# Down-projection of a streaming-encoder block: a ring of three weight chunks, one place for block sums, a fixed chunk order, and an end by products

## The chip, the cores and the metric

One core of a Trainium2 chip runs the whole kernel. The metric is device time in microseconds of one launch. The engines are TensorE (PE, with its weight loads PEld), VectorE (DVE), ScalarE (ACT), GpSimd (POOL) and SyncE (SP), which here only issues DMAs.

## What is computed

A block of a hybrid encoder on x of 512 frames by 1024: two attention branches, mixed into x, then a gated unit (ConvGLU) with its own residual. The change is in the last matrix product, `@ w_down`, of 2816 rows:

```python
def conv_glu(x, w_up, conv_w, conv_b, w_down):
    hid = x @ w_up
    ...
    gate, up = hid[..., :D_FF], hid[..., D_FF:]
    return (jax.nn.silu(gate) * up) @ w_down
...
x = x + conv_glu(rms_norm(x, norm2_g[l]), w_ffn_up[l], ...)
```

## The kernel before

Every product is done in float32 by three matmuls: each operand is split into a high part (a cast to a narrower type, by ScalarE: `hi`, tiles `whi`) and a residual (VectorE: `lo`, tiles `wlo`), and TensorE adds high x high, high x low and low x high. In `down_body` these are lines 855, 856 and 857.

The down-projection is done by Strassen's method in Winograd's form: 7 products in place of 8 block products. It has two sweeps, one for each half of 512 output columns, and in each sweep 11 chunks (`dn{s}_{i}`; sweep s, chunk i), one for each pair of 128-row blocks of `w_down`. The activation side (`pairs[i]`, tiles `a`) was made in the stage before. A chunk of weights has four raw blocks of 256 columns (128x1024, 512 KB), and three more blocks that are sums of them (`down_sums`, lines 111 to 113, VectorE). Three products take a raw block (1, 3 and 2), four take a sum (5, 7, 6 and 4). A chunk is 7 products x 2 row tiles x 3 = 42 matmuls, and each product adds up over the 11 chunks in a PSUM bank of its own; there are 8 banks.

How a chunk is prepared (`split_gen`): while TensorE works on chunk i, ScalarE casts chunk i+1 in two pieces (line 131: 768 columns of raw blocks, then 1024 with the sums), VectorE makes the two residuals (line 133), and SyncE then loads chunk i+2 (line 100). Raw tiles, `whi` and `wlo` have two buffers each. So a cast of chunk i+1 waits until TensorE has left chunk i-1, and a load waits until the residuals of two chunks before are done. A raw tile is 2048 wide: the left half holds the weights, the right half the chunk's own block sums.

At the end of a sweep (`fin`, `sweep`) the seven products are combined with x2, the block's input to this stage, which lies in DRAM (`x2d`). SyncE loads x2's columns for a sweep with chunk 6 of that sweep into one tile `xo` (line 870), VectorE adds the products to it as they end (line 884), in the order 1, 6, 5, 7, 2, 4, 3, and SyncE stores it (lines 878 and 915). Both sweeps use the same tile, so the loads of the second wait for the stores of the first.

A scheduler sets the order on each engine from the program's order and its own estimate of times; `behind(a, b)` forces a after b on one engine without a wait.

## Time and profile before

| | us |
|---|---|
| runs (3) | 748.29, 748.57, 749.75; median 748.57 |
| profiled execution | 750.49 |
| its span, first to last instruction | 747.8 |
| granted TensorE clock, mean | 0.996 |
| first matmul of the down-projection to its last (starts) | 626.3 to 740.5 |

The profile's columns are the engines' busy times. A row of the timeline has the start, the duration, engine, line, operation, tiles and shapes; in brackets stands the engine's idle time before it and what ended that. A row with x2 is two instructions with the sum of their time from the first's start to the last's end. The chain of waits leads back from the last instruction to what released each step.

### The profile page before, as it was taken

The page shows a single profiled execution, that of the slowest core. Times are in us where ns is not written, and L with a number is a line of the kernel's source. Part 1 is how long each engine was busy: PE and PEld are TensorE (multiplying, and loading weights), DVE is VectorE, ACT ScalarE, POOL GpSimd, SP SyncE. Part 2 cuts the span into 40 slices and gives each one's busy share as a digit, 9 for nine tenths or more (in the row PEclk, how much of TensorE's full clock was granted, in tenths as well). Part 3 has the DMA queues.
Part 4 walks back from the last instruction along what each step waited for, and adds up shares of the span by engine and source line. Part 5 has one row for each costly group of instructions (what it writes and reads, how often), then busy time and mean ns, then how long its engine had stood idle before and what let it go on. Part 6 is the DMA issues. An engine that isn't in the chain of part 4 may idle for free.

```text
span 747.8 us, 10959 instructions
## 1 busy us (share of the span) xinstructions
PE 733.1 (98%) x4301; PEld 645.1 (86%) x4301; DVE 536.0 (72%) x985; ACT 376.8 (50%) x671; POOL 41.8 (6%) x73
## 2 busy tenths in 40 slices
PE   9999999999999999999999999999999999998996
PEld 8999998888988888888899888888888889998896
DVE  6588876776978886573475777676668767878676
ACT  6675565557856775432254544534444433542341
POOL 2701200001011011000000000000000000000000
PEclk9999999999999999999999999999999999999999
DMA  8632232122221121235241232232133111443431
GB/s 295 250 122 85 79 116 74 61 88 79 65 106 57 57 99 71 85 113 224 114 169 61 110 112 75 96 112 103 67 113 113 61 53 57 141 142 122 159 109 62
DMA packets 19779, 79.96 MB, mean 107 GB/s; under 512 B 2192, under 2 KB 5392, under 8 KB 13584
## 3 DMA queue, kind: packets, MB, share of 16 engines
q1 hardware_dynamic: 19584, 79.18, 30.0%
q8 instruction: 33, 0.54, 0.3%
q14 instruction: 18, 0.15, 0.1%
q10 hardware_dynamic: 144, 0.10, 0.0%
HBM read 75.07 MB, written 4.19 MB: 106 GB/s over the span
## 4 chain that ended last, share of the span: by engine, by line
PE 89%; DMA 5%; DVE 4%; ACT 0%; SPq 0%; issue 0%; POOL 0%; ACTq 0%; DVEq 0%
PE pg L153 5%; PE pu L153 5%; PE pu L152 5%; PE pg L152 5%; PE pu L154 5%; PE pg L154 5%; PE P L856 3%; DMA raw_dn<-in_wdn 3%; PE P L857 3%; PE P L855 3%; PE gA L152 2%; PE wo L154 2%; PE wo L152 2%; PE wo L153 2%; PE gA L154 2%; PE qkB L152 2%
## 5 line engine op out<-in xcount | busy, mean ns | idle before, releaser
L133 DVE TENSOR_TENSOR wlo_up<-raw_up,whi_up 128x1024 fp32r<-128x1024 f32 (+1 forms) x50 | 52.4, 1093 | 49.6 <-ACT whi_up L131 49.6
L856 PE MATMUL P<-wlo_dn,a 128*128 128x256 f32 x308 | 83.2, 282 | 3.0 <-DVE wlo_dn L133 3.0
L857 PE MATMUL P<-whi_dn,a 128*128 128x256 f32 x308 | 82.8, 281 | 0.0
L855 PE MATMUL P<-whi_dn,a 128*128 128x256 f32 x308 | 76.6, 281 | 1.2 <-ACT whi_dn L131 1.2
L131 ACT CAST whi_dn<-raw_dn 128x768 fp32r<-128x768 f32 (+1 forms) x44 | 40.3, 943 | 63.2 <-PE P L857 38.2
L153 PE MATMUL pu<-htl,whi_up 128*128 128x512 f32 (+1 forms) x192 | 72.1, 375 | 0.0
L153 PE MATMUL pg<-htl,whi_up 128*128 128x512 f32 (+1 forms) x192 | 72.0, 375 | 0.0
L152 PE MATMUL pu<-hth,whi_up 128*128 128x512 f32 (+1 forms) x192 | 71.7, 374 | 0.0
L152 PE MATMUL pg<-hth,whi_up 128*128 128x512 f32 (+1 forms) x192 | 71.7, 374 | 0.0
L154 PE MATMUL pg<-hth,wlo_up 128*128 128x512 f32 (+1 forms) x192 | 71.1, 370 | 0.0
L154 PE MATMUL pu<-hth,wlo_up 128*128 128x512 f32 (+1 forms) x192 | 71.0, 370 | 0.0
L856 PEld LDWEIGHTS P<-wlo_dn,a 128*128 128x128 f32 x308 | 58.4, 191 | 3.5 <-DVE wlo_dn L133 3.4
L131 ACT CAST whi_up<-raw_up 128x1024 fp32r<-128x1024 f32 (+1 forms) x50 | 44.6, 945 | 29.9 <-PE pu L153 26.1
L857 PEld LDWEIGHTS P<-whi_dn,a 128*128 128x128 f32 x308 | 58.4, 191 | 0.0
L133 DVE TENSOR_TENSOR wlo_dn<-raw_dn,whi_dn 128x768 fp32r<-128x768 f32 (+1 forms) x44 | 47.6, 1088 | 12.3 <-ACT whi_dn L131 12.1
L855 PEld LDWEIGHTS P<-whi_dn,a 128*128 128x128 f32 x308 | 54.0, 190 | 2.2 <-ACT whi_dn L131 2.2
L152 PEld LDWEIGHTS pu<-hth,whi_up 128*128 128x128 f32 x192 | 36.0, 188 | 7.1
L152 PEld LDWEIGHTS pg<-hth,whi_up 128*128 128x128 f32 x192 | 36.0, 188 | 7.0
L154 PEld LDWEIGHTS pg<-hth,wlo_up 128*128 128x128 f32 x192 | 36.0, 188 | 6.7
L154 PEld LDWEIGHTS pu<-hth,wlo_up 128*128 128x128 f32 x192 | 36.0, 188 | 6.7
L153 PEld LDWEIGHTS pu<-htl,whi_up 128*128 128x128 f32 x192 | 36.1, 188 | 6.0
L153 PEld LDWEIGHTS pg<-htl,whi_up 128*128 128x128 f32 x192 | 36.1, 188 | 5.9
(239 smaller groups left out, 1922.0 us busy)
## 6 DMA issues: line engine op xcount, KB each, us to landing
raw_up<-in_wts SPq DMA_DIRECT2D x22, 1024.0 KB, 4.7
raw_dn<-in_wdn SPq DMA_DIRECT2D x22, 512.0 KB, 3.3
raw_gA<-in_wts SPq DMA_DIRECT2D x4, 1024.0 KB, 4.7
raw_qkB<-in_wts SPq DMA_DIRECT2D x4, 1024.0 KB, 4.7
raw_gB<-in_wts SPq DMA_DIRECT2D x4, 1024.0 KB, 4.7
raw_wo<-in_wts SPq DMA_DIRECT2D x4, 1024.0 KB, 4.7
xs<-in_xt SPq DMA_DIRECT2D x8, 256.0 KB, 4.6
xtok<-in_x SPq DMA_DIRECT2D x4, 512.0 KB, 8.4
```

The source lines that it names most:

```text
L131: A.copy(hi[:, sl], raw[:, sl])
L133: E.tensor_tensor(lo[:, sl], raw[:, sl], hi[:, sl].bitcast(F32), op=ALU.subtract)
L152: PE.matmul(ps, sh, mh, start=first, stop=False)
L153: PE.matmul(ps, sh, ml, start=False, stop=False)
L154: PE.matmul(ps, sl, mh, start=False, stop=last)
L855: PE.matmul(dst, sh, mh, start=first and t == 0, stop=False, skip_group_check=True)
L856: PE.matmul(dst, sh, ml, start=False, stop=False, skip_group_check=True)
L857: PE.matmul(dst, sl, mh, start=False, stop=last, skip_group_check=True)
```

## The change

- Three chunks of weights lie in a ring: the two raw tiles are cut into four quarters, three for weights, and the fourth (`ring[1][:, 1024:2048]`) for the block sums of whichever chunk is being split. Loads run three chunks ahead.
- The casts of all chunks stand in a fixed order on ScalarE, the residuals on VectorE (`late["casts"]`, `late["halves"]`).
- From chunk 5 of sweep 1 on, high and low parts go to buffers of activation pairs that are no longer used (tag `ap`), so that they do not wait for TensorE.
- The seam: sweep 0 combines its products without x2 in a tile `c`, partly by copies on ScalarE (`fin0`). The remaining eight adds and x2's loads are spread over sweep 1 (`rest0`), one add called for with each of chunks 1 to 6 while the next one is split, the last two at the end.
- Products are taken in the order 1, 2, 3, 6, 5, 7, 4, the three that need no sums first.
- The end: the last two chunks of sweep 1 are split before either is finished, and taken product by product (1, 6, 2, then 5, 7, 4, and 3 by row tiles), each combined as it ends. The last store goes out on ScalarE's queue.

```diff
 def load(i, parts=1):
     if i >= FIRST_DN:
+        j = (i - FIRST_DN) % 3
+        if i in (FIRST_DN, FIRST_DN + 2):
+            ring.append(wp.tile([P, 2048], F32, tag="raw", name=f"raw_dn{len(ring)}"))
+        raws[i] = ring[j // 2][:, j % 2 * 1024:(j % 2 + 1) * 1024]
+        SP.dma_start(raws[i], wdn[i - FIRST_DN])
-        SP.dma_start(raws[i][:, 0:1024], wdn[i - FIRST_DN])
...
 def down_sums(raw):
     b = raw.rearrange("p (b c) -> p b c", c=256)
-    V.tensor_tensor(b[:, 4:6], b[:, 0:4:2], b[:, 0:2][:, ::-1], op=ALU.subtract)
+    ts = ring[1][:, 1024:2048]
+    t = ts.rearrange("p (b c) -> p b c", c=256)
+    V.tensor_tensor(t[:, 0:2], b[:, 0:4:2], b[:, 0:2][:, ::-1], op=ALU.subtract)
...
+            if i >= FIRST_DN:
+                late["halves"] = (behind(ins, late.get("halves", ())),)
+                late["casts"] = (behind(cast, late.get("casts", ())),)
...
-    PRODS = (1, 6, 5, 7, 2, 4, 3)
+    PRODS = (1, 2, 3, 6, 5, 7, 4)
...
+    def rest0():
+        c, u, v = tmp["c"], tmp["u"], tmp["v"]
...
+        for t, (o, i) in enumerate(((v3(u), blk(c, 1, 1)), (blk(c, 0, 1), v3(v)),
+                                    (blk(c, 1, 1), v3(v)), (blk(c, 1, 0), v3(u)))):
+            get(t)
+            add(o, o, i, after=late["halves"])
+            yield
+        for t in range(NT):
+            add(c[:, t, :], c[:, t, :], x[:, t, :], after=late["halves"])
+            SP.dma_start(out[0, t * P:(t + 1) * P, 0:512], c[:, t, :])
+            yield
...
+    for s in range(2):
+        for i in range(NP - 2 * s):
...
+            for _ in run_chunk(f"dn{s}_{i}", down_body(s, i)):
+                pass
+    for _ in split_gen(pos[f"dn1_{NP - 1}"], 2):
+        pass
+    tmp["x"] = fetch("x_1", 512)
+    ends = [(i, splits.pop(f"dn1_{i}")) for i in (NP - 2, NP - 1)]
+    prev = ()
+    for ps in ((1, 6, 2), (5,), (7,), (4,)):
+        for i, (hi, lo) in ends:
+            for p in ps:
+                prev = product(1, p, i, hi, lo, prev=prev)
+                if i == NP - 1:
+                    fin1(p)
...
+    for t in range(2):
+        for i, (hi, lo) in ends:
+            prev = product(1, 3, i, hi, lo, (t,), prev)
+    fin1(3)
```

How this moves the instructions on VectorE is shown at three places. First, the middle of sweep 0, before (`wlo` rows are residuals, 768 wide for raw blocks and 1024 for sums; L111 to L113 are the three sums):

```order
L133 TENSOR_TENSOR wlo_dn0_8_6257<-raw_dn0_8_6161,whi_dn0_8_6256 128x768
L133 TENSOR_TENSOR wlo_dn0_8_6257<-raw_dn0_8_6161,whi_dn0_8_6256 128x1024
L111 TENSOR_TENSOR raw_dn0_9_6218<-raw_dn0_9_6218 128x512
L112 TENSOR_TENSOR raw_dn0_9_6218<-raw_dn0_9_6218 128x256
L113 TENSOR_TENSOR raw_dn0_9_6218<-raw_dn0_9_6218 128x256
L133 TENSOR_TENSOR wlo_dn0_9_6310<-raw_dn0_9_6218,whi_dn0_9_6309 128x768
L111 TENSOR_TENSOR raw_dn0_10_6271<-raw_dn0_10_6271 128x512
L133 TENSOR_TENSOR wlo_dn0_9_6310<-raw_dn0_9_6218,whi_dn0_9_6309 128x1024
```

and in the changed kernel, where L118 to L120 are the sums and L150 the residuals, and `raw_dn0` and `raw_dn1` are the two tiles of the ring:

```order
L150 TENSOR_TENSOR wlo_dn0_8_6246<-raw_dn1_5739,whi_dn0_8_6245 128x768
L118 TENSOR_TENSOR raw_dn1_5739<-raw_dn1_5739 128x512
L119 TENSOR_TENSOR raw_dn1_5739<-raw_dn1_5739 128x256
L120 TENSOR_TENSOR raw_dn1_5739<-raw_dn1_5739 128x256
L150 TENSOR_TENSOR wlo_dn0_8_6246<-raw_dn1_5739,whi_dn0_8_6245 128x1024
L150 TENSOR_TENSOR wlo_dn0_9_6298<-raw_dn0_5671,whi_dn0_9_6297 128x768
L118 TENSOR_TENSOR raw_dn1_5739<-raw_dn0_5671 128x512
L119 TENSOR_TENSOR raw_dn1_5739<-raw_dn0_5671,raw_dn1_5739 128x256
L120 TENSOR_TENSOR raw_dn1_5739<-raw_dn1_5739,raw_dn0_5671 128x256
L150 TENSOR_TENSOR wlo_dn0_9_6298<-raw_dn1_5739,whi_dn0_9_6297 128x1024
```

Before, the next chunk's first sum stands between the two residuals of a chunk, or its sums ahead of them; now a chunk's three sums stand between its own two residuals, and all go to one place in `raw_dn1`.

Second, VectorE in sweep 1, chunks 4 and 5, before:

```order
L111 TENSOR_TENSOR raw_dn1_4_6567<-raw_dn1_4_6567 128x512
L112 TENSOR_TENSOR raw_dn1_4_6567<-raw_dn1_4_6567 128x256
L113 TENSOR_TENSOR raw_dn1_4_6567<-raw_dn1_4_6567 128x256
L133 TENSOR_TENSOR wlo_dn1_4_6659<-raw_dn1_4_6567,whi_dn1_4_6658 128x768
L111 TENSOR_TENSOR raw_dn1_5_6620<-raw_dn1_5_6620 128x512
L133 TENSOR_TENSOR wlo_dn1_4_6659<-raw_dn1_4_6567,whi_dn1_4_6658 128x1024
L112 TENSOR_TENSOR raw_dn1_5_6620<-raw_dn1_5_6620 128x256
L113 TENSOR_TENSOR raw_dn1_5_6620<-raw_dn1_5_6620 128x256
L133 TENSOR_TENSOR wlo_dn1_5_6712<-raw_dn1_5_6620,whi_dn1_5_6711 128x768
L133 TENSOR_TENSOR wlo_dn1_5_6712<-raw_dn1_5_6620,whi_dn1_5_6711 128x1024
```

and now, where L881 is an add of the seam (`c` and `v` are its tiles) and `hl` a chunk's high and low parts in a buffer of the pairs:

```order
L150 TENSOR_TENSOR wlo_dn1_4_6631<-raw_dn0_5671,whi_dn1_4_6630 128x768
L118 TENSOR_TENSOR raw_dn1_5739<-raw_dn0_5671 128x512
L119 TENSOR_TENSOR raw_dn1_5739<-raw_dn0_5671,raw_dn1_5739 128x256
L120 TENSOR_TENSOR raw_dn1_5739<-raw_dn1_5739,raw_dn0_5671 128x256
L150 TENSOR_TENSOR wlo_dn1_4_6631<-raw_dn1_5739,whi_dn1_4_6630 128x1024
L881 TENSOR_TENSOR c_0_6186<-c_0_6186,v_0_6440 128x2x256
L150 TENSOR_TENSOR hl_dn1_5_6684<-raw_dn0_5671,hl_dn1_5_6684 128x768
L118 TENSOR_TENSOR raw_dn1_5739<-raw_dn0_5671 128x512
L119 TENSOR_TENSOR raw_dn1_5739<-raw_dn0_5671,raw_dn1_5739 128x256
L120 TENSOR_TENSOR raw_dn1_5739<-raw_dn1_5739,raw_dn0_5671 128x256
L150 TENSOR_TENSOR hl_dn1_5_6684<-raw_dn1_5739,hl_dn1_5_6684 128x1024
L881 TENSOR_TENSOR c_0_6186<-c_0_6186,u_0_6401 128x2x256
```

An add of sweep 0 now stands behind each chunk's second residual, and the sums again between the residuals.

Third, the end of VectorE's program, before (`P1_1` to `P7_1` are products 1 to 7 of sweep 1, `xo1` is the tile with x2):

```order
L133 TENSOR_TENSOR wlo_dn1_10_6979<-raw_dn1_10_6889,whi_dn1_10_6978 128x1024
L884 TENSOR_TENSOR xo1_6485<-P1_1_6486,xo1_6485 128x2x256
L884 TENSOR_TENSOR u2_1_7029<-P6_1_6500,u2_1_7029 128x512
L884 TENSOR_TENSOR u5_1_7045<-P5_1_6511,u2_1_7029 128x512
L884 TENSOR_TENSOR xo1_6485<-P2_1_6525,xo1_6485 128x2x256
L884 TENSOR_TENSOR xo1_6485<-u5_1_7045,xo1_6485 128x2x256 x2
L884 TENSOR_TENSOR u2_1_7029<-P7_1_6518,u2_1_7029 128x512
L884 TENSOR_TENSOR xo1_6485<-P3_1_6539,xo1_6485 128x256 x2
L884 TENSOR_TENSOR xo1_6485<-P7_1_6518,xo1_6485 128x2x256
L884 TENSOR_TENSOR xo1_6485<-u2_1_7029,xo1_6485 128x2x256
L884 TENSOR_TENSOR xo1_6485<-xo1_6485,P4_1_6532 128x2x256
```

and now, where `x_1` is the tile with x2:

```order
L150 TENSOR_TENSOR hl_dn1_10_6937<-raw_dn1_5739,hl_dn1_10_6937 128x1024
L881 TENSOR_TENSOR c_0_6186<-c_0_6186,x_0_6543 128x512 x2
L881 TENSOR_TENSOR x_1_6945<-P1_1_6456,x_1_6945 128x2x256
L881 TENSOR_TENSOR u_1_6974<-P6_1_6487,u_1_6974 128x512
L881 TENSOR_TENSOR x_1_6945<-x_1_6945,u_1_6974 128x2x256
L881 TENSOR_TENSOR x_1_6945<-P2_1_6470,x_1_6945 128x2x256
L881 TENSOR_TENSOR v_1_7009<-P5_1_6494,u_1_6974 128x512
L881 TENSOR_TENSOR x_1_6945<-x_1_6945,v_1_7009 128x2x256 x2
L881 TENSOR_TENSOR x_1_6945<-P7_1_6501,x_1_6945 128x2x256 x2
L881 TENSOR_TENSOR x_1_6945<-x_1_6945,P4_1_6508 128x2x256
L881 TENSOR_TENSOR x_1_6945<-P3_1_6480,x_1_6945 128x256 x2
```

The last chunk's residual is followed by two adds of sweep 0, then by those of sweep 1 in the order of the products; before, the residual was followed by the adds of its own sweep alone.

More of the change, by code (lines that the diff above doesn't have):

```diff
@@ new lines, in fin1, with put @@
+    def fin1(p):
+        ps = banks[1][p]
+        x = tmp["x"]
+        def put(r, c):
+            for t in range(2 * r, 2 * r + 2):
+                SP.dma_start(out[0, t * P:(t + 1) * P, 512 + 256 * c:768 + 256 * c], x[:, t, 256 * c:256 * (c + 1)])
+        if p == 1:
+            tmp["u"] = fp.tile([P, S], F32, tag="cg", name="u_1", bufs=1)
+            behind(A.copy(tmp["u"], ps), late["casts"])
+            add(blk(x, 0, 0), v3(ps), blk(x, 0, 0), after=late["halves"])
+        elif p == 6:
+            add(tmp["u"], ps, tmp["u"])
+        elif p == 2:
+            add(blk(x, 0, 0), v3(ps), blk(x, 0, 0))
+            put(0, 0)
+        elif p == 5:
+            tmp["v"] = fp.tile([P, 768], F32, tag="st", name="v_1", bufs=1)[:, 0:S]
+            add(tmp["v"], ps, tmp["u"])
+            add(blk(x, 1, 1), blk(x, 1, 1), v3(tmp["v"]))
+            add(blk(x, 0, 1), blk(x, 0, 1), v3(tmp["v"]))
+            add(blk(x, 1, 0), blk(x, 1, 0), v3(tmp["u"]))
+        elif p == 7:
+            add(blk(x, 1, 1), v3(ps), blk(x, 1, 1))
+            put(1, 1)
+            add(blk(x, 1, 0), v3(ps), blk(x, 1, 0))
+        elif p == 4:
+            add(blk(x, 1, 0), blk(x, 1, 0), v3(ps), op=ALU.subtract)
+            put(1, 0)
+        else:
+            for t in range(2):
+                o = x[:, t, 256:512]
+                add(o, ps[:, 256 * t:256 * (t + 1)], o)
+                (SP, A)[t].dma_start(out[0, t * P:(t + 1) * P, 768:1024], o)
```

183 lines of the change are left out of this document (92 added, 91 removed).

## The prediction

> **What bounds the kernel now.** I read the page's busy row first, then a table by stage, then TensorE's timeline, the chain of waits, and VectorE's and ScalarE's timelines.
>
> ```profile
> PE 733.1 (98%) x4301; PEld 645.1 (86%) x4301; DVE 536.0 (72%) x985; ACT 376.8 (50%) x671; POOL 41.8 (6%) x73
> 680.00:690.00 10.00, 7.77 (x57) 7.47 (x56) 10.00 (x20) 1.89 (x2) 0.00 (x0) 0.87 0.37 113
> 690.00:700.00 10.00, 9.42 (x76) 9.01 (x75) 6.34 (x9) 3.48 (x4) 0.00 (x0) 0.96 0.60 195
> 700.00:710.00 10.00, 9.23 (x81) 9.03 (x80) 6.18 (x10) 3.67 (x4) 0.00 (x0) 1.00 0.41 153
> 687.40:690.81 3.41, 3.26 (x15) 3.26 (x16) 3.22 (x8) 0.00 (x0) 0.00 (x0) 0.50 0.64 187
> ```
>
> TensorE is busy for 98% of the span, so only idle time, pace and the end are left to win. In the table (in us: stretch, then busy time of PE, PEld, VectorE, ScalarE, POOL, granted clock, DMA) the seam between the two sweeps, 680 to 710, has all that is missing: 2.23, 0.58 and 0.77 us, and a granted clock of 0.87 and 0.96, which is one stretch at 0.50 (its 15 matmuls took 3.26 us). Before the down-projection nothing changes: the instructions up to its first chunk stand in the same order on every engine.
>
> ```profile
> 637.24 0.74 PE L855 MATMUL P<-whi_dn,a 128*128 128x256 f32 x4 [0.33 <-ACT whi_dn L131]
> 687.55 0.58 PE L856 MATMUL P<-wlo_dn,a 128*128 128x256 f32 x1 [2.23 <-DVE wlo_dn L133]
> 706.00 0.39 PE L856 MATMUL P<-wlo_dn,a 128*128 128x256 f32 x1 [0.77 <-DVE wlo_dn L133]
> 740.50 0.28 PE L857 MATMUL P<-whi_dn,a 128*128 128x256 f32 x1
> ...
> 691.03 4.03 DMA out<-xo
> 695.20 0.33 SPq L870
> 697.00 6.38 DMA raw_dn<-in_wdn
> 703.47 0.70 DVE raw_dn L111
> ```
>
> TensorE waits 2.23 us at the seam for VectorE's residual, which is queued behind the sums of the sweep's end; and 0.77 us at 706.0 for a residual whose weights came late. The chain shows why late: the output stores (691.0) hold SyncE's x2 loads (695.2), and these hold the next weight load (697.0 to 703.4). After 706.0 the chain is TensorE alone to its last matmul at 740.50, then VectorE and the stores, to the span's end at 747.8.
>
> Two paces occur without any wait. A chunk is 42 matmuls, and ScalarE's cast of a chunk starts when TensorE releases the buffer of two chunks back (the first row is the weight load of a chunk, 3.3 us to land):
>
> ```profile
> raw_dn<-in_wdn SPq DMA_DIRECT2D x22, 512.0 KB, 3.3
> ...
> 661.63 1.79 ACT L131 CAST whi_dn<-raw_dn 128x768 fp32r<-128x768 f32 x2 [2.21 <-PE P L857]
> 666.39 1.79 ACT L131 CAST whi_dn<-raw_dn 128x768 fp32r<-128x768 f32 x2 [2.97 <-PE P L857]
> 721.08 0.83 ACT L131 CAST whi_dn<-raw_dn 128x768 fp32r<-128x768 f32 x1 [2.65 <-PE P L857]
> 726.02 0.83 ACT L131 CAST whi_dn<-raw_dn 128x768 fp32r<-128x768 f32 x1 [2.63 <-PE P L857]
> ```
>
> 666.39 - 661.63 = 4.76 us, and 726.02 - 721.08 = 4.94 us, 113 and 118 ns a matmul, both at a granted clock of 1.00. What sets the pace I can't read; I use both as ends.
>
> **The change, part by part.** *What it can remove.* The waits on DMA: three chunks of weights are held, so a load leaves about two chunk periods (9.5 us) before its use, against its 3.3; the x2 loads of sweep 0 move into sweep 1 and its stores into the middle of sweep 1. On SyncE the moved x2 loads wait for TensorE's first chunk of sweep 1, with the load of chunk 4 queued behind them; that chunk is cast some 9 us later, so this costs nothing; without that cover it would cost up to a chunk period. The seam's adds are cut to three, and four copies on ScalarE, which is half idle. If TensorE alone set the end, the starts of its matmuls give the gain: 2.2 + 0.6 + 0.8 idle, 1.6 for the halved clock (3.26 - 15 x 0.113), and at the end 3.6 (7.3 now from the last matmul's start; then 0.3 to the add, 0.4 for it and 2.9 to close, worked out below): 8.8 us. It does not, because of what follows.
>
> *What it adds.* Block sums now have one place for all chunks, and VectorE's order is fixed: residual of the direct part, three sums, then the residual of the sums, and only then the next chunk. So the three sums of the next chunk can no longer fill the wait for ScalarE's cast of these sums. The costs, start to start, are in sweep 1 of the present kernel:
>
> ```profile
> 712.32 0.69 DVE L111 TENSOR_TENSOR raw_dn<-raw_dn 128x512 f32<-128x512 f32 x1 [1.50 <-DMA raw_dn<-in_wdn]
> 713.05 0.42 DVE L112 TENSOR_TENSOR raw_dn<-raw_dn 128x256 f32<-128x256 f32 x1
> 713.51 0.42 DVE L113 TENSOR_TENSOR raw_dn<-raw_dn 128x256 f32<-128x256 f32 x1
> 713.85 0.95 DVE L133 TENSOR_TENSOR wlo_dn<-raw_dn,whi_dn 128x768 fp32r<-128x768 f32 x1
> 714.72 0.68 DVE L111 TENSOR_TENSOR raw_dn<-raw_dn 128x512 f32<-128x512 f32 x1
> 715.32 1.22 DVE L133 TENSOR_TENSOR wlo_dn<-raw_dn,whi_dn 128x1024 fp32r<-128x1024 f32 x1
> 716.46 0.42 DVE L112 TENSOR_TENSOR raw_dn<-raw_dn 128x256 f32<-128x256 f32 x1
> ...
> 713.97 1.05 ACT L131 CAST whi_dn<-raw_dn 128x1024 fp32r<-128x1024 f32 x1 [0.72 <-DVE raw_dn L113]
> ...
> 732.60 1.05 ACT L131 CAST whi_dn<-raw_dn 128x1024 fp32r<-128x1024 f32 x1 [0.79 <-DVE raw_dn L113]
> 733.68 1.23 DVE L133 TENSOR_TENSOR wlo_dn<-raw_dn,whi_dn 128x1024 fp32r<-128x1024 f32 x1 [0.25 <-ACT whi_dn L131]
> ```
>
> Direct residual to the next instruction 0.87 (713.85 to 714.72); first sum to second 0.73; second to third 0.46; third to the cast 0.46 (713.51 to 713.97); cast to its residual 1.08 (732.60 to 733.68); that residual to the next 1.14 (715.32 to 716.46). Sum: **4.73 us a chunk** on VectorE, of which 1.08 is waiting. TensorE needs 4.76 to 4.94. In sweep 0 this just holds, with TensorE as the bound, but VectorE gains no lead.
>
> In sweep 1 each of chunks 2 to 7 gets one of the seam's adds behind its last residual. An add costs 0.60:
>
> ```profile
> 684.47 1.29 DVE L884 TENSOR_TENSOR xo<-u,xo 128x512 f32<-128x512 f32 x2
> 685.68 0.68 DVE L884 TENSOR_TENSOR u<-P,u 128x512 f32<-128x512 f32 x1
> ```
>
> (two from 684.47 to 685.68). 4.73 + 0.60 = **5.33 us**, more than TensorE's 4.76 to 4.94: VectorE becomes the bound, and TensorE waits about 0.4 to 0.6 us per chunk. At the end it waits more: by products, the sums of chunk 9 and of chunk 10 are both wanted within about 3 us, and VectorE makes them 4.73 us apart.
>
> *The sum along VectorE.* The chain starts where both kernels still agree, at the first residual of chunk 3 of sweep 0:
>
> ```profile
> 639.22 2.09 DVE L133 TENSOR_TENSOR wlo_dn<-raw_dn,whi_dn 128x768 fp32r<-128x768 f32 x2
> 743.79 0.69 DVE L884 TENSOR_TENSOR xo<-xo,P 128x512 f32<-128x512 f32 x1
> 743.19 2.12 SPq L878 DMA_DIRECT2D out<-xo  x4
> out<-xo SPq DMA_DIRECT2D x16, 128.0 KB, 1.9
> ```
>
> 639.2 is set by ScalarE's cast of chunk 2 and so by TensorE, with the same instructions ahead. Chunk 3: 0.87, first sum 0.60, a last residual of the activations 0.87 (as the direct one, 768 columns), 0.46 + 0.46 + 1.08 + 1.14, that is 5.48: chunk 4 begins at 644.7. Seven chunks of 4.73 to the first of sweep 1: 677.8. That chunk has three adds in or behind it and the next one's first sum: 4.73 + 4 x 0.60 = 7.13, to 684.9. Chunk 1 without its first sum: 4.73 - 0.73 = 4.00, to 688.9. Six of 5.33: 720.9. Two of 4.73: 730.4. Chunk 10: 735.1. Then two adds of sweep 0 and ten of sweep 1 at 0.60, two of which wait 0.11 for the one before, and two halves, 0.33 and 0.42: 735.1 + 7.2 + 0.2 + 0.75 = 743.3 as the end of the last add. Now it is 743.79 + 0.69 = 744.5, and the span ends 3.3 us later: two stores one behind the other (0.4 each on SyncE), 1.9 us to land, 1.0 to close. Now one of them goes out on ScalarE's queue, so 0.4 less: 743.3 + 2.9 = **746.2 us** against 747.8, a gain of 1.6.
>
> TensorE's own end must lie under that. The residual of chunk 10 is done at 735.2 and 59 matmuls are left, 6.7 to 6.9 us: its last start is at 742.1 at the latest, the end of its add 0.3 + 0.4 later, 742.8. It fits with 0.5 us to spare, at full clock. With TensorE's slow pace in sweep 0 the cast releases, not VectorE, set the seam, some 0.7 us later: the sum has 0 to +0.7 from that; I take the lower, since the fast pace here begins with the wait for a cast at 637.24, which stays.
>
> *The clock.* Ahead of those 59 matmuls TensorE waits for chunk 10's cast and residual: the residual of chunk 9's sums is done at 725.6 + 3.6 + 1.2 = 730.4, the 17 matmuls behind it take 2.0, and chunk 10's follows at 735.2, so some 2.5 of 2.8 us are idle. What such a stretch does to the clock:
>
> ```profile
> 683.99:687.40 3.41, 1.33 (x10) 1.11 (x9) 3.41 (x5) 0.18 (x1) 0.00 (x0) 1.00 0.00 0
> 704.47:707.88 3.41, 2.64 (x23) 2.44 (x22) 3.38 (x6) 1.78 (x2) 0.00 (x0) 1.00 0.01 2
> 738.60:742.00 3.40, 2.18 (x19) 1.97 (x17) 3.28 (x6) 0.00 (x0) 0.00 (x0) 1.00 0.23 77
> ```
>
> These stretches follow the 3.41 us steps in which the trace's clock changes. The first, with 1.33 us busy, was followed by the one at half clock; those with 2.64 and 2.18 busy were followed by full clock. A step that covers the 2.8 us would have about 1 us busy, under 1.33; about half of the ways in which the steps can lie do so. Then TensorE loses 3.41 x 0.5 = 1.7 us in the last 59 matmuls, ends 1.7 - 0.5 = 1.2 us past VectorE, and the span is 747.4.
>
> The Trainium skill, page "TensorE: Matmul & The Clock Gate", section "What's actually happening", says that the window is free-running and that the clock halves after at least one idle window of about 3.4 us. By that rule waits of 1.5 and 1.0 us never halve it, and the end stays at 746.2; the trace does not agree, since 2.08 idle of 3.41 did.
>
> **Own time and the runs.** The profiled execution took 750.5 us (span 747.8 and 2.7 around it), the runs 748.3 to 749.8, median 748.6. The gain of 1.6 (no halving) or 0.4 (halving) is from the span; the two have about even chances. I put it on the median and take 1.0, between them: **747.6 us**.
>
> **Rivals.** *A, TensorE stays the bound.* If VectorE's chain were shorter, say the cast wait overlapped, the gain would near the 8.8 us above: 739.8 us; half of it, 744.2. For it: VectorE is only 72% busy. Against: the rows above have hardly any spread, and the order on VectorE leaves nothing to put into the wait. 0.15, mostly near 744.2.
>
> *B, VectorE's chain is longer than its parts: slower.* The place is the first sum of each chunk: it writes over sums that the residual before it has read, in the tile that also holds every third chunk of weights. If that is held until VectorE's preceding instruction ends, or the cast and residual see more latency than 1.08, each chunk of the 19 pays. It decides from (1.6 + 1.5) / 19 = 0.16 us a chunk, where the time is 1.5 us over the median; at 0.2 it costs 3.8, and the time is 748.6 - 1.6 + 3.8 = **750.8**. For it: a sum that follows its source costs 0.73 and not 0.60, so such holds exist. Against: the earlier residual ended 0.9 us before. 0.2.
>
> *C, the change doesn't do what it says:* the seam's wait goes but an equal one comes back elsewhere, by the halved clock and the slow pace together: 1.6 - 1.2 - 0.7 = -0.3, **748.9**. 0.05.
>
> **How the numbers follow.** The forecast, VectorE the bound, has 0.6, with its own range 746.6 to 748.6. About 0.2% (1.5 us) is what a measurement can't tell from no change: 747.1 to 750.1. Of the forecast's 0.6 about 0.2 is faster than that, 0.38 within, 0.02 slower; A is 0.15 faster; B 0.18 slower and 0.02 within; C 0.05 within. Faster 0.35, within 0.45, slower 0.20. The range takes in the near half of A and most of B: 744.3 to 750.9.
>
> **What would show it.** Right: no wait of VectorE for a weight load behind 640 us; the seam's 2.23 gone; 4.73 us between the direct residuals in sweep 0 and 5.33 in chunks 3 to 7 of sweep 1; TensorE waiting for ScalarE's casts there, and over 2 us in all before the last products; the last add near 743.3. Wrong: a lead of VectorE in sweep 1 with TensorE closed up (A), a period over 4.9 in sweep 0 (B), or a halved clock after 735 with the last add near 744.5, which moves the time by 1.2 inside the forecast.

## The result, and the profile after

The changed kernel takes 749.62 us in the median of 12 runs (748.62 to 750.53), the kernel before 748.65 (12 runs, 747.37 to 749.75): a ratio of 1.0011, interval [1.0003, 1.0020]. It is 1.0 us slower where the forecast had it 1.0 us faster, at 747.6. That lies inside the range given and inside what was called no change, but on the other side of it. The profiled execution took 749.92 us, its span is 748.2.

The same table by stage as shown of before, now of the changed kernel (in us: stretch, then busy time of PE, PEld, VectorE, ScalarE, POOL, granted clock, DMA), with two 3.41 us steps of the clock at the end:

```profile
PE 737.1 (99%) x4301; PEld 648.2 (87%) x4301; DVE 536.8 (72%) x984; ACT 377.3 (50%) x674; POOL 41.8 (6%) x73
680.00:690.00 10.00, 10.00 (x87) 10.00 (x87) 7.67 (x13) 5.02 (x7) 0.00 (x0) 1.00 0.34 100
690.00:700.00 10.00, 10.00 (x86) 9.69 (x85) 7.62 (x12) 3.58 (x4) 0.00 (x0) 1.00 0.62 217
700.00:710.00 10.00, 10.00 (x81) 9.43 (x80) 7.63 (x12) 3.57 (x4) 0.00 (x0) 1.00 0.30 102
732.49:735.90 3.41, 1.35 (x9) 0.95 (x8) 2.28 (x4) 1.53 (x2) 0.00 (x0) 1.00 0.00 0
735.90:739.31 3.41, 3.41 (x19) 3.41 (x18) 3.06 (x5) 0.00 (x0) 0.00 (x0) 0.50 0.41 154
```

The seam is closed: TensorE is busy for 10.00 us of each 10, where it was 7.77, 9.42 and 9.23, and the granted clock there is 1.00. Its share of the span went from 98 to 99%. Yet it does fewer matmuls in 700 to 710 (81) than in 680 to 690 (87): waits of some 0.2 us do not show as idle time, because the ends of matmuls are modelled. And the stretch at half clock is there again, now at 735.9. VectorE's timeline of one chunk in sweep 1, and of the end:

```profile
715.67 0.95 DVE L150 TENSOR_TENSOR hl_dn<-raw_dn,hl_dn 128x768 fp32r<-128x768 f32 x1
716.54 0.68 DVE L118 TENSOR_TENSOR raw_dn<-raw_dn 128x512 f32<-128x512 f32 x1
717.26 0.43 DVE L119 TENSOR_TENSOR raw_dn<-raw_dn,raw_dn 128x256 f32<-128x256 f32 x1
717.72 0.42 DVE L120 TENSOR_TENSOR raw_dn<-raw_dn,raw_dn 128x256 f32<-128x256 f32 x1
719.26 1.23 DVE L150 TENSOR_TENSOR hl_dn<-raw_dn,hl_dn 128x1024 fp32r<-128x1024 f32 x1 [1.11 <-ACT hl_dn L148]
720.40 0.69 DVE L881 TENSOR_TENSOR c<-c,x 128x512 f32<-128x512 f32 x1
721.00 0.95 DVE L150 TENSOR_TENSOR hl_dn<-raw_dn,hl_dn 128x768 fp32r<-128x768 f32 x1
...
735.19 1.28 DVE L881 TENSOR_TENSOR c<-c,x 128x512 f32<-128x512 f32 x2
...
739.88 0.69 DVE L881 TENSOR_TENSOR v<-P,u 128x512 f32<-128x512 f32 x1 [0.88 <-PE P L877]
...
744.19 0.75 DVE L881 TENSOR_TENSOR x<-P,x 128x256 f32<-128x256 f32 x2 [0.30 <-PE P L877]
```

Chunk 7's direct residual starts at 715.67, chunk 8's at 721.00: 5.33 us, with 1.11 of waiting for the cast of the sums ahead of 719.26 and the add (720.40) behind the second residual. Chunk 10's last residual is over at 735.19. After that VectorE waits for TensorE (0.88 and 0.30 us), as in the forecast's case with a halved clock. TensorE's timeline says why:

```profile
729.34 0.38 PE L875 MATMUL P<-hl_dn,a 128*128 128x256 f32 x1 [0.22 <-ACT hl_dn L148]
730.60 0.39 PE L876 MATMUL P<-hl_dn,a 128*128 128x256 f32 x1 [0.88 <-DVE hl_dn L150]
734.06 0.38 PE L875 MATMUL P<-hl_dn,a 128*128 128x256 f32 x1 [1.18 <-ACT hl_dn L148]
735.32 0.39 PE L876 MATMUL P<-hl_dn,a 128*128 128x256 f32 x1 [0.88 <-DVE hl_dn L150]
...
743.87 0.28 PE L877 MATMUL P<-hl_dn,a 128*128 128x256 f32 x1
```

It waits for the cast and the residual of chunk 9's sums, then for those of chunk 10's (start to start 1.26, 1.46 and 1.26 us ahead of the rows at 730.60, 734.06 and 735.32), then goes at half speed for one step, and starts its last matmul at 743.87, where it was 740.50. The span ends 3.3 us behind the last add.

The starts of the 924 matmuls of the down-projection give the account. 923 intervals at the fast pace of 113.3 ns are 104.6 us; what lies above that is sorted by the length of the interval: up to 127 ns a slower pace, in the step at half clock the clock, else a wait.

| us | before | changed | changed, second profile (below) | two places (below) | all combined (below) |
|---|---|---|---|---|---|
| waits | 6.4 | 8.0 | 7.8 | 2.1 | 2.0 |
| slower pace at full clock | 1.9 | 3.6 | 3.9 | 3.8 | 0.7 |
| halved clock | 1.4 | 1.6 | 0 | 0 | 0 |
| first start to last start | 114.2 | 117.8 | 116.3 | 110.5 | 107.3 |
| last start to the span's end | 7.3 | 4.3 | 4.8 | 4.6 | 4.4 |

So the seam's waits went and more came back in sweep 1 and at the end; the pace gave away another 1.7 us; the tail is 2.9 shorter. 114.2 + 7.3 = 121.5 us before, 117.8 + 4.3 = 122.1 after. The table says where TensorE's time lies, not what each row costs: where another engine sets the end, a faster matmul would only wait longer.

### The profile page after: what moved, and what is told of

Its sections match the earlier page's. It is cut to its first block, busy times and chain, and to the rows that moved or that the text cites. A ratio compares the mean times of both kernels' runs of the same rounds, so it can differ in the third digit from the quotient of the medians.

```text
span 748.2 us, 10982 instructions
## 1 busy us (share of the span) xinstructions
PE 737.1 (99%) x4301; PEld 648.2 (87%) x4301; DVE 536.8 (72%) x984; ACT 377.3 (50%) x674; POOL 41.8 (6%) x73
## 4 chain that ended last, share of the span: by engine, by line
PE 90%; DVE 5%; ACT 2%; issue 2%; DMA 1%; SPq 0%; DVEq 0%
PE pg L176 5%; PE pu L176 5%; PE pu L175 5%; PE pg L175 5%; PE pu L177 5%; PE pg L177 5%; PE P L876 3%; PE P L877 3%; PE P L875 3%; PE gA L175 2%; PE wo L176 2%; PE wo L177 2%; PE wo L175 2%; PE gA L177 2%; PE qkB L175 2%; PE gB L175 2%
## 5 line engine op out<-in xcount | busy, mean ns | idle before, releaser
L150 DVE TENSOR_TENSOR wlo_up<-raw_up,whi_up 128x1024 fp32r<-128x1024 f32 (+1 forms) x50 | 52.4, 1094 | 51.0 <-ACT whi_up L148 51.0
L876 PE MATMUL P<-wlo_dn,a 128*128 128x256 f32 x224 | 59.2, 281 | 0.0
L877 PE MATMUL P<-whi_dn,a 128*128 128x256 f32 x224 | 59.0, 280 | 0.0
L875 PE MATMUL P<-whi_dn,a 128*128 128x256 f32 x224 | 50.3, 282 | 0.5 <-ACT whi_dn L148 0.5
L148 ACT CAST whi_dn<-raw_dn 128x768 fp32r<-128x768 f32 (+1 forms) x32 | 29.1, 942 | 42.8 <-DVE raw_dn L120 38.2
L150 DVE TENSOR_TENSOR wlo_dn<-raw_dn,whi_dn 128x768 fp32r<-128x768 f32 (+1 forms) x32 | 34.2, 1089 | 20.6 <-ACT whi_dn L148 20.5
L876 PEld LDWEIGHTS P<-wlo_dn,a 128*128 128x128 f32 x224 | 42.3, 189 | 0.3
L877 PEld LDWEIGHTS P<-whi_dn,a 128*128 128x128 f32 x224 | 42.3, 189 | 0.0
L875 PEld LDWEIGHTS P<-whi_dn,a 128*128 128x128 f32 x224 | 36.6, 188 | 1.2 <-ACT whi_dn L148 1.2
```

The lines of the kernel that those rows point to most:

```text
L148: cast = A.copy(hi[:, sl], src)
L150: ins = E.tensor_tensor(lo[:, sl], src, hi[:, sl].bitcast(F32), op=ALU.subtract)
L875: behind(PE.matmul(dst, sh, mh, start=first and t == 0, stop=False, skip_group_check=True), prev)
L876: PE.matmul(dst, sh, ml, start=False, stop=False, skip_group_check=True)
L877: prev = (PE.matmul(dst, sl, mh, start=False, stop=last, skip_group_check=True),)
```

## Experiments

**Is it VectorE's chain?** In the first experiment a second place for the sums breaks it. It lies in the part of x's tile (`x_0`, tag `ap`) that x does not fill; `sums` holds the place already filled for the next chunk, and `down_sums` takes the place as an argument and puts the sums in VectorE's order behind the direct residual.

```diff
+            ts = sums.pop(i) if i in sums else down_sums(raw)
...
+            if j == 0 and FIRST_DN + NP + 2 <= i < len(order) - 1:
+                odd = (i - FIRST_DN - NP) % 2 == 0
+                sums[i + 1] = down_sums(raws[i + 1], late["x_0"][:, 2048:3072] if odd else None, True)
...
```

> In the changed kernel, but from chunk 3 of sweep 1 on the block sums alternate between two places and the sums of the next chunk are made between a chunk's two residuals, in the time of the cast. Theory (the one place makes VectorE wait 1.1 us a chunk for the cast and so bound sweep 1 and the end): VectorE's period falls from 5.33 to 0.87 + 0.73 + 0.46 + 0.46 + 1.14 + 0.60 = 4.26 us, under TensorE's 4.76 to 4.94; TensorE's waits from 698 us to the end, 8.0 us in the changed kernel, fall under 1.5 and its clock isn't halved (1.6); last matmul at 735.5 to 737, time 741 to 743 us. Rival (TensorE only trades one wait for another: weights, buffers, or a slower pace): the waits come back as waits for a weight load or for a buffer, or over 118 ns a matmul, and the time stays over 746.

Measured: 742.35 us (741.97 to 743.19), ratio 0.9918 [0.9903, 0.9933] to the kernel before. A chunk of sweep 1 on VectorE:

```profile
707.24 0.95 DVE L154 TENSOR_TENSOR hl_dn<-raw_dn,hl_dn 128x768 fp32r<-128x768 f32 x1
708.11 0.68 DVE L118 TENSOR_TENSOR x<-raw_dn 128x512 f32<-128x512 f32 x1
708.83 0.43 DVE L119 TENSOR_TENSOR x<-raw_dn,x 128x256 f32<-128x256 f32 x1
709.29 0.43 DVE L120 TENSOR_TENSOR x<-x,raw_dn 128x256 f32<-128x256 f32 x1
709.63 1.22 DVE L154 TENSOR_TENSOR hl_dn<-raw_dn,hl_dn 128x1024 fp32r<-128x1024 f32 x1
710.76 0.69 DVE L888 TENSOR_TENSOR c<-c,x 128x512 f32<-128x512 f32 x1
711.37 0.95 DVE L154 TENSOR_TENSOR hl_dn<-raw_dn,hl_dn 128x768 fp32r<-128x768 f32 x1
```

No wait is left, and 711.37 - 707.24 = 4.13 us a chunk. TensorE's last matmul starts at 736.04, its waits in the whole down-projection are 2.1 us, none of them behind 698 (in the changed kernel 6.8 of the 8.0 lie there, not all 8.0 as the expectation has it), and the clock is not halved. The theory holds, with a period even a little shorter than its 4.26. The place and the order changed together here, because the new order needs the second place. The slower pace stays as it was (3.8 us), which is the part of the rival that holds.

**What of the chain is the adds?** The second experiment leaves the one place and moves the six adds of chunks 2 to 7 into the wait for the cast.

```diff
+            if j == 0 and FIRST_DN + NP + 2 <= i < FIRST_DN + NP + 8:
+                late["halves"] += (late["sum"],)
+                next(late["rest"])
...
```

> In the changed kernel, but the seam's adds of chunks 2 to 7 stand between the third block sum and the residual of the sums, where VectorE waits for the cast, and no longer behind that residual. Theory (5.33 us a chunk is 4.73 plus an add): the period in sweep 1 is 4.73, chunk 10's residual of the sums ends 6 x 0.60 = 3.6 us earlier, TensorE loses no time in chunks 3 to 8 but still waits about 4 us before the last products; last matmul near 740.3, time 745.5 to 746.5. Rival (the wait isn't VectorE's to fill: the add delays the cast or the residual): period still over 5.1, time within 0.7 of the changed kernel's.

Measured: 746.30 us (744.74 to 746.93), ratio 0.9967 [0.9956, 0.9978]. The timeline shows the add ahead of the residual of the sums, and half of the wait left:

```profile
709.09 0.43 DVE L120 TENSOR_TENSOR raw_dn<-raw_dn 128x256 f32<-128x256 f32 x1
709.43 0.69 DVE L884 TENSOR_TENSOR c<-c,x 128x512 f32<-128x512 f32 x1
710.62 2.10 DVE L150 TENSOR_TENSOR hl_dn<-raw_dn,hl_dn 128x1024 fp32r<-128x1024 f32 x2 [0.51 <-ACT hl_dn L148]
...
713.82 0.42 DVE L120 TENSOR_TENSOR raw_dn<-raw_dn,raw_dn 128x256 f32<-128x256 f32 x1
714.16 0.68 DVE L884 TENSOR_TENSOR c<-c,x 128x512 f32<-128x512 f32 x1
715.36 2.10 DVE L150 TENSOR_TENSOR hl_dn<-raw_dn,hl_dn 128x1024 fp32r<-128x1024 f32 x2 [0.51 <-ACT hl_dn L148]
```

From third sum to third sum 713.82 - 709.09 = 4.73. The adds cost nothing there, and 3.3 us come back of the 3.6 that they cost behind the residual. The waits at the end stay (1.45 and 1.26 us), as does the halved clock.

**Does the spreading matter?** If VectorE bounds all of sweep 1, it does not matter where in it the adds stand.

```diff
-                if s == 1 and p == PRODS[2] and i < 7:
-                    next(rest, None)
+                if s == 1 and p == PRODS[2]:
+                    for _ in range({1: 4, 5: 1, 6: 1}.get(i, 0)):
+                        next(rest, None)
```

> The changed kernel, but the seam's four adds behind chunks 2 to 5 of sweep 1 stand together ahead of chunk 3's second sum (the two that add x stay behind chunks 6 and 7). Theory (VectorE bounds the whole of sweep 1, so where the adds stand is the same): TensorE waits some 2 us once in chunk 3 and little in chunks 4 and 5, chunk 10's residual of the sums ends where it did (735.3 less the run's own start), the end is as before, and the time is the changed kernel's within 0.5 us: 749.1 to 750.1. Rival (spreading them is what the change brings): the wait in chunk 3 is lost for good, time 751 to 752.5.

Measured: 748.90 us (748.37 to 750.07), ratio 1.0003 [0.9994, 1.0013]. TensorE's one long wait ahead of the end:

```profile
698.90 1.36 PE L875 MATMUL P<-whi_dn,a 128*128 128x256 f32 x7 [1.48 <-ACT whi_dn L148]
```

1.48 us for a cast, 1.75 from start to start. The chain's end and the waits behind it are the same. The median is 0.7 us under the changed kernel's first one, a little more than foreseen, but it comes from another chip, where the kernel before took 748.99; against that kernel it is no gain and no loss. So spreading the adds brought nothing here.

**What does the end by products bring?** Here only chunk 10 is taken in the order of the end, and chunk 9 is worked off whole.

```diff
-        for i in range(NP - 2 * s):
+        for i in range(NP - s):
...
-    ends = [(i, splits.pop(f"dn1_{i}")) for i in (NP - 2, NP - 1)]
+    ends = [(i, splits.pop(f"dn1_{i}")) for i in (NP - 1,)]
...
```

The edit also fixes the last two adds behind product 4's, the order that they have in the changed kernel.

> In the changed kernel, but chunk 9 of sweep 1 is worked off whole like the others, and only chunk 10 by the products' order of the end. Theory (with sums 4.73 us apart, the end by products makes TensorE wait): TensorE has chunk 9's 42 matmuls to do while VectorE makes chunk 10's sums, so the waits of 1.26, 1.46 and 1.26 us before the last products nearly go, the clock isn't halved, the last matmul is near 740.5; VectorE's adds then set the end near 743.3, and the time is 1 to 1.6 us under the changed kernel's. Rival (the end by products is what hides the adds): last add later than 744.9, time 0.5 to 2 over the changed kernel's.

Measured: 748.19 us (747.64 to 750.10), ratio 0.9995 [0.9984, 1.0007], 1.4 under the changed kernel run beside it. Of the four waits at the end (0.50, 1.26, 1.46 and 1.26 us from start to start) one of 0.43 and one of 1.26 are left, the clock is not halved ahead of the last matmul, and VectorE sets the end:

```profile
734.48 0.39 PE L876 MATMUL P<-hl_dn,a 128*128 128x256 f32 x1 [0.88 <-DVE hl_dn L150]
...
741.12 0.69 DVE L881 TENSOR_TENSOR x<-x,P 128x512 f32<-128x512 f32 x1
741.73 0.75 DVE L881 TENSOR_TENSOR x<-P,x 128x256 f32<-128x256 f32 x2
```

No bracket stands behind the last adds, so VectorE has no wait there, and ends them at 742.48. The last matmul starts at 738.66, earlier than the 740.5 expected. The theory holds: the end by products cost 1.4 us in the median, though the ranges overlap (747.96 to 751.28 with it). From the first matmul to the span's end the profiles have 120.7 us here, and 121.1 and 122.1 in the changed kernel without and with a halved step.

**Does the idle time halve the clock, and what does that cost?** Ten matmuls that nobody reads fill part of the wait.

```diff
+            if i == NP - 1 and ps[0] == 1:
+                for k in range(10):
+                    a9, h9 = pairs[NP - 2], ends[0][1][0]
+                    prev = (behind(PE.matmul(idle[:, 0:256], a9[:, 0:P], h9[:, 0, :], ...), prev),)
...
```

This edit, too, fixes the last two adds behind product 4's.

> The changed kernel with ten more matmuls (into a bank that nobody reads) between chunk 9's first three products and chunk 10's, where TensorE waits 1.46 and then 1.26 us: 10 x 0.12 = 1.2 us of them are filled, nothing is computed otherwise. Theory (the clock is halved by the idle time in the 3.4 us step before, which costs about 1.2 us at the end): no step at half clock behind the waits in any profile, and a median 0.6 to 1.2 us under the changed kernel's of the same call (not every run of that is halved). Rival (the halving doesn't hang on these waits, or VectorE's adds set the end anyway): the same median within 0.3.

> The changed kernel beside the one with filled waits, for the comparison on one chip. 749.6 within 0.8; a third profile that tells whether the paces and the halved clock return.

Measured: 748.24 us (747.59 to 749.96) with filled waits, 749.35 (748.29 to 751.71) without, 12 runs each on one chip. The step that holds the waits, and the one behind it, in the table by stretches:

```profile
731.19:734.60 3.41, 2.71 (x21) 2.34 (x19) 2.23 (x4) 1.63 (x2) 0.00 (x0) 1.00 0.00 0
734.60:738.01 3.41, 3.23 (x27) 3.23 (x28) 3.41 (x7) 0.00 (x0) 0.00 (x0) 1.00 0.41 154
```

With 2.71 us busy of 3.41 the next step is granted 1.00; in the changed kernel above 1.35 busy gave 0.50. A second profile of the changed kernel, taken for the next question, has the same waits, but there they fall on two steps, and neither is followed by half clock:

```profile
730.24:733.65 3.41, 2.24 (x18) 1.93 (x16) 2.23 (x5) 1.39 (x2) 0.00 (x0) 1.00 0.00 0
733.65:737.07 3.42, 2.54 (x21) 2.46 (x21) 3.38 (x6) 0.14 (x1) 0.00 (x0) 1.00 0.31 116
```

All 12 runs with filled waits have a mean clock of 0.999 or 1.000. Of the 12 without, two have 1.000 (748.29 and 748.37), four 0.998 and six 0.996 or 0.997 (749.1 and 750.3 us in the median). The two profiles with a halved step have 0.996 and 0.997, and the one without 0.998 (it was at half clock only behind its last matmul). By that about half of the runs are halved, and the theory holds: filling the waits takes 1.1 us off the median. In the profiles, from the first matmul of the down-projection to the span's end, it is 122.1 us twice with a halved step, 121.1 without, and 120.8 with filled waits. So the halved step itself costs 1.0 us.

**Where does the pace come from?** A second profile of the changed kernel, and two edits of the kernel with two places, each for one of the stretches at 118 and 120 ns. The first moves a residual of the activations into the wait for chunk 3's cast in sweep 0, so that TensorE does not wait there. The second gives chunks 5 to 9 of sweep 1 the tiles `whi` and `wlo` again.

> The changed kernel once more. If the matmuls' pace (113, 118 or 120 ns at full clock) belongs to the program, the stretches of 645 to 688 us at 118 ns and 688 to 698 at 113 ns come back, and so does the halved clock behind 735; if chance at a restart of TensorE sets it, they lie elsewhere and the last matmul's start moves by up to 2 us (924 matmuls by 5 ns is 4.6). Time 749.6 either way within 0.8.

```diff
+            if j == 0 and i == FIRST_DN + 3:
+                low = V.tensor_tensor(*late["a10"], op=ALU.subtract)
+                late["halves"] = (behind(low, late["halves"] + (late["sum"],)),)
...
```

> The kernel with two places for sums, in which the last residual of the activations (0.87 us on VectorE, ahead of chunk 3's second sum in sweep 0) stands in the wait for the cast of chunk 3's sums. Theory (a wait of 0.18 us at matmul 25 of chunk 3 of sweep 0 restarts TensorE in the slow pace, and it keeps that pace until the next wait): the wait goes, the chunks from 3 of sweep 0 to the seam take 4.76 us and not 4.95, 9 x 0.19 = 1.7 us less: 740.3 to 741.1 us. Rival (the pace goes with something else, the places of the operands for one): chunks 4 to 10 keep 4.95 us and the time stays within 0.4 of 742.35.

```diff
-            if i < FIRST_DN + NP + 5:
+            if i < FIRST_DN + NP + 10:
...
```

> The kernel with two places for sums, in which chunks 5 to 9 of sweep 1 keep the two high and two low tiles of the chunks before, and only chunk 10 has a tile of its own that holds both its high and its low part. Theory (120 ns a matmul goes with the tile that holds both parts: it begins at chunk 5 in every run so far): chunks 5 to 9 run at 113 or 118 ns, 210 x 2 to 7 ns = 0.4 to 1.4 us less, and chunk 10 at 120; time 741 to 742. Rival (120 ns comes from elsewhere): chunks 5 to 9 at 5.04 us again; or TensorE waits for casts that wait for its buffers, and the time is 742.5 to 744.

Measured: 749.57 us (747.96 to 751.28) for the changed kernel again, 741.50 (740.93 to 744.14) for the first edit, 741.33 (740.72 to 742.36) for the second, against 742.35 with two places alone. The two edits ran on another chip than two places alone; the kernel before had 748.70 and 748.61 on the two. The rows are stretches of four whole chunks, 168 matmuls (the counts take in those that run across an edge): chunks 4 to 7 of sweep 0 in the changed kernel, again, and with the residual moved; then chunks 6 to 9 of sweep 1 with two places alone, and 5 to 8 in the tiles of before:

```profile
646.72:666.51 19.79, 19.79 (x171) 19.79 (x169) 14.41 (x21) 7.78 (x9) 0.00 (x0) 1.00 0.32 107
```
```profile
645.99:665.78 19.79, 19.79 (x170) 19.79 (x169) 14.42 (x21) 7.76 (x9) 0.00 (x0) 1.00 0.33 107
```
```profile
648.88:667.92 19.04, 19.04 (x170) 19.04 (x169) 14.18 (x20) 7.33 (x9) 0.00 (x0) 1.00 0.35 111
```
```profile
710.96:731.12 20.16, 20.16 (x170) 20.16 (x169) 16.01 (x24) 5.77 (x7) 0.00 (x0) 1.00 0.37 131
```
```profile
706.82:725.86 19.04, 19.04 (x171) 19.04 (x169) 16.84 (x25) 8.94 (x10) 0.00 (x0) 1.00 0.45 154
```

19.79, 19.79 and 19.04 us; 20.16 and 19.04: 117.8, 113.3 and 120.0 ns a matmul, all at a granted clock of 1.00. The slow stretch in sweep 0 came back at the same matmul, the 27th of chunk 3, behind an interval of 0.19 us; the stretch of 688 to 698 us at 113 ns did not come back in the second profile, where it stayed at 118, nor did the halved clock. In the first edit, without that wait, TensorE went on at 113.3 ns to the seam. And 120 ns goes with the tile that holds both parts: in the second edit chunk 10, which keeps such a tile, is back at 120 ns right behind chunk 9's matmuls at 113, with no wait between. That tile is also a buffer of the activation pairs, so these runs do not tell the sharing from the place. Both theories hold, the first size does not: sweep 0 ends 1.5 us earlier, but 0.5 us are given back in waits for VectorE in chunks 0 and 1 of sweep 1, so 0.9 of the 1.7 is left in the median, and 1.1 in the profile from the first matmul to the span's end (114.0 against 115.1). The second saves 1.4 us of pace in the profile and 1.0 in the median.

**The last store's queue**, on the kernel with two places:

```diff
-                (SP, A)[t].dma_start(out[0, ...], o)
+                SP.dma_start(out[0, ...], o)
```

> The kernel with two places for sums, but both last stores go out on SyncE, as in the kernel before. If ScalarE's queue saves the 0.4 us that the prediction took, the span's end lies 0.4 us further behind the last add (now 3.5) and the time is 742.7 to 742.8; if it saves nothing, the time is the same within 0.2.

Measured: 742.68 us (742.60 to 743.24), 0.33 over the 742.35 (741.97 to 743.19) of two places with both queues, but the ranges overlap and the chips differ. The profiles have the last store on ScalarE's queue, and then both on SyncE:

```profile
737.15 0.36 ACTq L971 DMA_DIRECT2D out<-x  x1
```
```profile
737.32 0.89 SPq L971 DMA_DIRECT2D out<-x  x2
```

With both queues the last store is issued 0.03 us behind the end of the last add (737.12), and the span ends 3.51 behind that add. With one queue it is issued 0.50 behind it (737.31), and the span ends 3.60 behind it. So in these profiles the earlier issue is worth 0.1 us and not 0.4. The rest of what the two profiles differ by lies ahead of the last add, 0.4 us from the first matmul to there, where the instructions are the same.

**How long is the kernel before?**

> The kernel before, once more, to see how much of its profiled execution's 747.8 us of span belongs to that execution. Theory (the prediction's start was a long execution): the first matmul of the down-projection starts up to 1 us before 626.26, the span is near 746.3, and the halved clock at the seam and the paces of 113 ns in sweep 0 and 118 ns from chunk 4 of sweep 1 are there again. Rival: the first matmul at 626.2 and a span of 747.5 to 748 again, so that the loss lies in the changed part alone.

Measured: 749.11 us, span 747.4, first matmul of the down-projection at 626.02, the halved clock at the seam again, 113 ns from chunk 2 of sweep 0 on, 118 ns from chunk 2 of sweep 1. From the first matmul to the span's end these are 121.4 us, as in the first profile (121.5). That is the rival's side. But the spans of its other runs are shorter than both profiles: the median is 746.4 in the 21 runs beside the first four experiments, 746.9 in the 22 beside the filled waits. This stays between the two.

**Together**, with one more edit: of the first sums in the second place, one stands ahead of chunk 2's residual and two behind it.

```diff
+                for op in (ops[j:1 + 2 * j] if i == FIRST_DN + NP + 2 else ops[3 * j:]):
+                    late["sum"] = behind(op(), late["halves"])
+                    late["halves"] = (late["sum"],)
...
```

> Two places for sums from chunk 3 of sweep 1 on, the activations' last residual in the wait for a cast, chunks 5 to 9 of sweep 1 in the tiles of the chunks before, and, new, the first sums in the second place split: one ahead of chunk 2's residual of the sums, in the wait for the cast, two behind it (in the kernel with two places all three stood ahead, and TensorE waited 0.51 and some 0.4 us in chunk 2). If the gains add: 742.35 - 0.9 (pace of sweep 0, less what the seam gives back) - 1.0 (pace of chunks 5 to 9) - 0.7 (chunk 2) = 739.7, within 739.0 to 740.5 us. If a faster TensorE only meets VectorE's residuals at the seam: 741 or more.

Measured: 739.25 us (738.43 to 740.24), ratio 0.9879 [0.9860, 0.9899]: 9.7 us under the kernel before on that chip, and the best of all. The gains add: from the first matmul to the span's end the profiles have 115.1 us with two places alone and 111.7 here.

## Why the prediction was wrong, and where it was right

*The mechanism was right: VectorE became the bound.* 4.73 us a chunk in sweep 0 and 5.33 in chunks 2 to 7 of sweep 1 are what the trace shows; the direct residual of chunk 8 starts at 721.00 (forecast 720.9), chunk 10's last residual ends at 735.19 (735.1). VectorE waits for no weights, and the 2.23 us of the seam are gone. Taking the chain apart gave 7.2 us (two places) and 3.3 (adds in the wait) against the changed kernel run beside them, so this bound is shown. It is also where most of the 8.8 us went that the change could remove: two places alone come to 6.3 us under the kernel before (742.35 against 748.61), although TensorE's pace loses 1.9 us more there; the combination, with the pace won back, reaches rival A's 739.8.

*The step that failed is the end of the sum along VectorE, "743.3 + 2.9", with the half clock's end behind it; and then "Own time and the runs".* Counted from the first matmul of the down-projection (626.26 in the forecast's execution), the forecast's two ends, 746.2 and 747.4, are 119.9 and 121.1 us, 1.6 and 0.4 under the 121.5 of before. Measured: 121.1 without the halved step (second profile, from 625.33), 122.1 with it. So the gains were +0.4 and -0.6, 1.2 and 1.0 under the forecast. The rows say where, as what was measured less what was forecast:

| us | not halved | halved |
|---|---|---|
| chain to chunk 10's last residual | +0.3 | +0.3 |
| from there, or from TensorE's end, to the end of the last add | +0.2 | +0.4 |
| from the last add to the span's end | +0.7 | +0.4 |

VectorE's rows for it in the second profile (those of the first are shown above):

```profile
734.48 1.28 DVE L881 TENSOR_TENSOR c<-c,x 128x512 f32<-128x512 f32 x2
...
742.12 0.75 DVE L881 TENSOR_TENSOR x<-P,x 128x256 f32<-128x256 f32 x2
```

The last residual is over at 734.48, 109.15 us behind the first matmul, where the forecast has 735.1 - 626.26 = 108.84; the last add ends at 742.87. The last row of the table is the largest. The forecast took 0.4 off because the second of two stores no longer stands behind the first on SyncE. The stores of the changed kernel's last 14 us, with their time to land:

```profile
out<-x SPq DMA_DIRECT2D x7, 128.0 KB, 1.9
out<-x ACTq DMA_DIRECT2D x1, 128.0 KB, 2.1
```

and the last rows of ScalarE's queue in the changed kernel, and of SyncE's in its second profile:

```profile
744.97 0.35 ACTq L964 DMA_DIRECT2D out<-x  x1
```
```profile
743.14 0.40 SPq L964 DMA_DIRECT2D out<-x  x1
```

The store on ScalarE's queue leaves at 744.97, 0.03 behind the last add, so the 0.4 are saved at that point; but it lands in 2.1 us and not 1.9, and the span ends 3.3 us behind the add, as before. With two places, both stores on SyncE made the tail only 0.1 us longer, so the term of 0.4 is the one that was mis-sized. In the second profile the store of the first half leaves SyncE only at 743.14, 0.27 behind the last add (742.87), with six stores ahead of it: 3.6. In the middle row the halved case had 0.7 from the last matmul's start to the end of the add, and took 1.07: the row at 744.19 shows that both halves of the last add waited for the last matmul, where the sum had one of them done before. Not halved, three adds wait for the one before and not two.

These 1.0 to 1.2 us are half of the 2.0 by which the forecast missed, or a little more. The rest, 0.8 to 1.0, lies between profiles and runs: "I put it on the median" takes it that the runs differ from the profiled execution by the same in both kernels. The kernel before's runs have spans of 746.4 to 747.1 in the medians of four groups, 0.7 to 1.4 under its first profile; the changed kernel's have 747.5 to 747.9 in three, 0.3 to 0.7 under its first. What makes that difference was not traced, and it stays open. It does not go with the clock of the kernel before: its runs with a mean clock of 0.998 or 0.999 (20 of 63) have the same median span as the others, 746.8.

The even chance for a halved step was about right, and so was its price, 1.2: it is 1.0 in the profiles (122.1 against 121.1), and of the changed kernel's 34 runs the 15 with a mean clock of 0.996 or 0.997 have a median span of 748.5, the others 747.3. One slip changes nothing: the end's share of the 8.8 us is 7.3 - 3.6 = 3.7, not 3.6, and the sum of the unrounded terms is 8.8. TensorE's last 59 matmuls ran at 120 ns and not at the 113 to 118 of the sum, 7.05 us without the halved step where 6.7 to 6.9 were taken; the 0.5 us to spare covered that.

*What sets the pace* was left open, with 0 to +0.7 for the seam and the lower end taken. The seam came 0.1 us late (685.00 against 684.9), so it cost this kernel nothing, since VectorE's chain sets the end; but once that is broken each of the two slow stretches is worth about 1 us.

*The rivals.* A did not happen in this kernel, where VectorE has no lead in sweep 1; with the second place VectorE got that lead, and the time was 742.35. B is refuted: the period in sweep 0 is 4.73, not 4.9. C, given 0.05, came nearest with its 748.9, and half by its mechanism: the waits did come back elsewhere and the halved clock with them, while the slow pace did not matter. That the time lies inside the range given is no support for the sum, which had the sign of the change wrong.

*The clock rule.* The Trainium skill, page "TensorE: Matmul & The Clock Gate", section "What's actually happening", has the clock halve after at least one idle window of about 3.4 us. By it, read as a window without any matmul, neither kernel would be halved here, and filling the waits would have changed nothing. The runs differ: 1.35 us busy of 3.41 were followed by 0.50, 2.71 by 1.00. That the windows run free of the program, as the same section says, agrees: the second profile has the same waits (1.26, 1.45 and 1.26 us from start to start), but they fall on two steps with 2.24 and 2.54 us busy, and no step is halved.

## What to carry to other kernels

Before a shared buffer and a fixed order go in, add up the engine's chain with its waits on other engines, and compare it with the bound engine's period. Where it is longer, look for a second place or for an instruction to move into the wait: here they were worth 7.2 and 3.3 us, while the change without them gained nothing. A gain worked out from one profiled execution belongs to that execution: before it is put on the runs, compare its span with theirs. A short wait on TensorE can cost more than its length, by the pace or the clock behind it.

## What the runs showed of the hardware

- At a granted clock of 1.00 the same matmuls (128x256, with a weight load each) have three steady paces, 113.3, 117.8 and 120.0 ns. A wait can switch between the first two, and the pace then lasts until the next longer interval, which can be very short: in chunk 1 of sweep 1 the changed kernel's first profile went back to 113 ns behind an interval of 0.125 us, while the second stayed at 118 behind one of 0.127. The wait's length does not decide: behind an interval of 0.60 to 0.61 us in chunk 2 of sweep 0, where all twelve profiles of changed kernels have the same instructions, TensorE went on at 113 ns in eleven and at 118 in the one with the seam's adds together.
- 120 ns came in each changed kernel with the first chunk whose high and low part share a tile (chunk 5 of sweep 1), and went when they were in two tiles of the weights. Whether the sharing or the place of the tile does it is open.
- The half clock follows a step of 3.41 us with few matmuls, not only one with none. In all fourteen profiles, from 622 us on and in steps counted from the trace's own changes of the clock, each step of full clock in which at most ten matmuls (of 256 columns) started was followed by half clock, and each with fourteen or more by full clock. With twelve it went both ways: 1.73 us busy was followed by half clock, 1.61 and 1.69 by full clock.
- An add that reads the first half of a bank waited for the last matmul into its other half: in the changed kernel the last matmul starts at 743.87 and both adds run from 744.19 on, though the first half's own last matmul started six matmuls earlier. Whether the program's own wait or the chip asks for that is open.
